# Parameter-only work of a state-space recurrence, moved into steps beside the feed-forward layer ahead of it, with its results in DRAM scratch

## The chip, the core and the metric

The kernel runs on one core of a Trainium2 chip. The metric is device time in microseconds (us) from launch to end. Three runs of the kernel before took 2534.7, 2537.55 and 2545.49 us; their median is 2537.55. The core's engines are named as in its profile: PE (TensorE, matrix multiplication), DVE (VectorE), ACT (ScalarE), POOL (GpSimd) and SP (SyncE, which issues most DMAs). Each works through its own instruction list in order and waits on semaphores where it needs another engine's result.

## The reference, cut to what matters

Two blocks of two layers each work on 512 tokens of 1024 features. The first block ends with a feed-forward layer (FFN) with a short convolution. The second block's first layer mixes a causal attention with forgetting and a diagonal state-space recurrence (S5); experts and a second mixer follow and are not touched.

```python
def _conv_ffn(x, norm_g, w_up, conv_w, conv_b, w_down):
    h = _rmsnorm(x, norm_g)
    up = h @ w_up                      # 1024 -> 2 * 2816
    gate, val = up[..., :D_FF], up[..., D_FF:]
    gate = conv3(gate, conv_w) + conv_b
    return (jax.nn.silu(gate) * val) @ w_down

def fox_s5_mixer(x, w_in, f_bias, a_re, a_im, log_dt, b_re, b_im, c_re, c_im, d_skip, w_glu, b_glu, w_out):
    q, k, v, f_logit, u = split(x @ w_in)
    att = forgetting_attention(q, k, v, f_logit + f_bias)
    y = s5_scan(u, a_re, a_im, log_dt, b_re, b_im, c_re, c_im, d_skip)
    y = jax.nn.gelu(y)
    y = y * jax.nn.sigmoid(y @ w_glu + b_glu)
    return jnp.concatenate([att, y], axis=-1) @ w_out

def s5_scan(u, a_re, a_im, log_dt, b_re, b_im, c_re, c_im, d_skip):
    dt = jnp.exp(log_dt)[:, None]
    mag = jnp.exp(a_re * dt)
    lb_re, lb_im = mag * jnp.cos(a_im * dt), mag * jnp.sin(a_im * dt)
    ...                                # z = (lb - 1) / a, bb = z * b, complex
    bu = einsum('bsgc,gpc->bsgp', u, bb)
    h = scan of h[t] = lb * h[t-1] + bu[t]
    y = einsum(h_re, c_re) - einsum(h_im, c_im)
    return y + d_skip * u
```

Everything in `s5_scan` down to `bb`, and every product of powers of lb with b or c, depends on parameters alone.

## The kernel before, in words

The program goes layer by layer: two mixers with an FFN behind each (f0, f1; f1 is "the second FFN"), then x0 (attention and S5), experts, a third mixer, experts. Features lie on partitions and the 512 tokens along the free dimension. Every product of two fp32 matrices is three matmuls of split operands: hi times hi, hi times lo, lo times hi (`mm3`, L153 to L155). `K.weight` (L140) loads a weight of up to 1 MB on SP's queue into one of two raw buffers; ACT makes its hi part in three pieces (whi, L147), and DVE or POOL in turn its lo part (wlo, L148). There are two buffers for hi and lo.

The FFN (function `ffn`) splits its normalised input into xh and xl, and computes 22 chunks of 128 gate and 128 value features, 48 matmuls of 128x512 each; after 11 chunks, 8 down products. Gate sums go to PSUM banks mm, value sums to sc, two banks of each kind. Per chunk DVE takes gt (mm times the row factor rb, L332), two taps of the convolution into y, v (sc times rb, then times y) and the lo split hl. rb comes from rms: PE sums squares, DVE makes rms and diag (L245), PE spreads it, ACT copies it as rb (L250).

The layer x0 (function `layer2`) takes tiles from a pool of 42 units of 128x512 and six tiles k4 of 128x1024. Its parts are generators that are woven by count: one side takes its steps of the other in proportion. On one side stand `s5_states` (parameters first: powers PW, phases, Er and Ei, bb and bs, four W by quads with PE transposes into Wt; then states) and eight steps of `s5_outputs` (four CP by quads, on POOL for quads 0 and 2 and on DVE for 1 and 3; then Kc by PE, 64 small matmuls at L1359 and L1360, which is copied out by ACT, and spread by 32 DMAs into the Toeplitz tiles T). On the other side stand the products of the layer: inputs u, forget gates, values, queries and keys (copied out of PSUM as fqk, L189). The state's outputs are hs (L1158 within a stacked complex product). After the weave PE does attention scores and the outputs' matmuls, T times U and CP times hs (L1380, L1381).

The order of instructions on each engine is not written by hand: a list scheduler places them by program order as priority, by its own estimates of time, and by when a buffer of a pool is free. An engine then executes that order as it stands.

Of the kernel before, what the change touches and what calls it, by code (L numbers as in the profile page):

```python
# [27 lines left out]
class Ctx:  # L28
# [137 lines left out]
    def rsqrt(self, v, n, name="rs"):  # L166
        """v: AP [P, n] fp32 (SBUF, > 0); returns tile [P, n] with v ** -0.5"""
# [17 lines left out]
    def copy(self, out, in_):  # L185
        """a copy out of PSUM, on ScalarE or (turns) by turns on ScalarE and VectorE"""
# [6 lines left out]
    def rsqrt_wide(self, ps, scale, eps):  # L193
        """(ps * scale + eps) ** -0.5 as an SBUF tile [P, 512]; ps in PSUM"""
# [10 lines left out]
    def silu2(self, x):  # L205
        """x <- 2 x / (1 + exp(-x)) = x (1 + tanh(x / 2)) of an SBUF tile; tanh shares a table with exp"""
# [4 lines left out]
    def sumsq_add(self, acc, src, first):  # L211
        """acc[P, 512] += src ** 2"""
# [8 lines left out]
    def colsum(self, acc):  # L221
        """column sums over partitions of acc [P, 512], as [P tokens, 4] in PSUM"""
# [5 lines left out]
    def rms_cols(self, acc, n, eps):  # L228
        """(column sums / n + eps) ** -0.5 as columns [P tokens, 4]; a step of Newton's method makes up for what the square root lacks"""
# [10 lines left out]
    def row_bcast(self, cols, name):  # L240
        """cols [P tokens, 4] -> SBUF tile [P, 512] holding the value of each token in every partition"""
# [11 lines left out]
    def split_into(self, hi, lo, src, scale=None, eng=None):  # L253
        """hi + lo = src * scale (scale: None or an AP [P, 1])"""
# [10 lines left out]
def weave(*parts):  # L265
    """runs generators side by side; parts: (generator, its number of steps)"""
# [15 lines left out]
def split_g(K, xT, g):  # L282
    """hi and lo tiles of xT * g; xT: 8 tiles [P, 512], g [P, 8]"""
# [9 lines left out]
def norm_cols(K, xT):  # L293
    """1 / rms(x) of 8 tiles [P, 512], as columns [P tokens, 4]"""
# [6 lines left out]
def norm_split(K, xT, g):  # L301
    """hi and lo tiles of xT * g, and the columns 1 / rms(x) [P tokens, 4]; the tiles of xT come one after the other"""
# [8 lines left out]
def ffn(K, xT, w_up, conv_w, conv_b, w_down, norm_g, tag):  # L311
    """xT (8 tiles [P, 512]) += conv_ffn(rmsnorm(xT)), in place.
    w_up [22, P, 2048] (8 k, gate 128 | val 128), conv_w [P, 22 * 3], conv_b [P, 22], w_down [2, 8, P, 1408], norm_g [P, 8]"""
# [5 lines left out]
    rb = K.row_bcast(rc, "rb")  # L319
    for half in range(2):  # L320
        hh, hl = [], []
        for j in range(11):
            f = half * 11 + j
            wh, wl = K.weight(w_up[f], 2048, nc.gpsimd if f < 2 else None)
# [22 lines left out]
        for d in range(8):  # L347
# [14 lines left out]
def lay_down(w):  # L362
    """[2816, 1024] -> [2, 8, 128, 1408]"""
# [3 lines left out]
def lay_col(v):  # L367
    """[n * 128] -> [128, n]"""
# [9 lines left out]
def sincos(K, sin, cos, ang, tmp):  # L378
    """sin and cos of ang (tiles or APs of one shape; tmp: three more, the first int32). ang is overwritten"""
# [12 lines left out]
def rope_tables(K, pos, inv):  # L392
    """pos [P, 4] int32, inv [P, 48]: sin and cos tiles [P, 4, 48] (16 columns for the 32-wide heads, 32 for the 64-wide)"""
# [15 lines left out]
def proj_T(K, src, n, nk, xh, xl):  # L409
    """src: DRAM [P, nk * n * 128] chunk, or hi and lo of one; yields PSUM tiles [P out, 512 tokens]"""  # L410
# [10 lines left out]
def proj_N(K, src, n, xh, xl):  # L421
    """src: DRAM [P, nk * n] chunk; yields t and the PSUM tile [P tokens, n] of each group of 128 tokens"""
# [12 lines left out]
def proj_few(K, src, n, xh, xl):  # L435
    """src: DRAM [P, 8 * n], n <= 128; the PSUM tile [n, 512 tokens]"""
# [7 lines left out]
def bc(ap, n):  # L444
    """[P, a] -> [P, a, n], the values repeated along the last axis"""
# [1824 lines left out]
```

## Time and profile before

| What | Value |
|---|---|
| runs, us | 2534.7, 2537.55, 2545.49 (median 2537.55) |
| profiled execution: span, us | 2542.8, first to last instruction |
| its own time | not given apart; at least the span |
| PE busy | 2292.3 us, 90% |
| DVE, ACT, POOL busy | 1488.8 (59%), 1064.3 (42%), 795.6 us (31%) |
| mean granted clock of PE | 0.946 |
| second FFN, about | 1032 to 1395 us |
| x0 up to the last key matmul | 1395 to 1566 us |

The trace is of one execution. Times in it count from its first instruction. A clock of 1.00 is PE's upper level, 2.4 GHz. "Idle before" is the time in which an engine stood still ahead of an instruction, with the one that released it.

### The profile page before, as it was taken

How to read it: one execution, taken by the hardware profiler on the slowest of the kernel's cores; microseconds unless marked ns; L12 is line 12 of the kernel's file. 1: busy time of each engine (PE TensorE's matmuls, PEld its weight loads, DVE VectorE, ACT ScalarE, POOL GpSimd, SP SyncE). 2: the span in 40 equal slices, each digit the busy share in tenths (PEclk: the TensorE clock that was granted, in tenths of full speed). 3: DMA queues.
4: the chain of work that ended last, by engine and by line, in shares of the span. 5: the costliest groups of instructions: out<-in, count | busy, mean ns of one | idle time of the engine just before them, and what ended most of it. 6: DMA issues, size and time to landing. Idle time of an engine off the chain costs nothing. (4 is left out here: it accounts for less than half of the span.)

```text
span 2542.8 us, 32031 instructions
## 1 busy us (share of the span) xinstructions
PE 2292.3 (90%) x12404; PEld 1858.3 (73%) x12404; DVE 1488.8 (59%) x2713; ACT 1064.3 (42%) x1802; POOL 795.6 (31%) x582
## 2 busy tenths in 40 slices
PE   7999899999998999999999978995985899997892
PEld 6845658888886988788888866675875788886781
DVE  6256756525545447752554784657765545576766
ACT  4233455323334323532333223534665444445563
POOL 5321203222222322322222151216543312154444
PEclk9999899999998999999999998996988899998996
DMA  3111202223221121223222212124986322245883
GB/s 142 67 35 35 76 1 83 89 95 107 84 93 67 67 67 67 83 89 101 100 84 91 71 40 67 51 99 157 326 308 221 119 83 77 73 176 210 298 321 139
DMA packets 59432, 289.89 MB, mean 114 GB/s; under 512 B 12576, under 2 KB 13600, under 8 KB 33664
## 3 DMA queue, kind: packets, MB, share of 16 engines
q1 hardware_dynamic: 48944, 265.51, 30.0%
q0 software_dynamic: 6912, 16.79, 1.9%
q10 hardware_dynamic: 3408, 5.39, 0.6%
q8 instruction: 101, 1.65, 0.3%
q14 instruction: 67, 0.55, 0.1%
HBM read 271.79 MB, written 23.07 MB: 116 GB/s over the span
## 5 line engine op out<-in xcount | busy, mean ns | idle before, releaser
L148 POOL TENSOR_TENSOR wlo<-wraw,whi 128x683 fp32r<-128x683 f32 (+8 forms) x317 | 557.2, 1785 | 1266.2 <-ACT whi L147 1215.6
L147 ACT ACTIVATE whi<-wraw 128x683 fp32r<-128x683 f32 (+9 forms) x627 | 474.3, 818 | 386.5 <-PE mm L154 127.1
L148 DVE TENSOR_TENSOR wlo<-wraw,whi 128x683 fp32r<-128x683 f32 (+9 forms) x310 | 342.8, 1144 | 90.0 <-ACT whi L147 83.5
L153 PE MATMUL mm<-xh,whi 128*128 128x512 f32 (+2 forms) x576 | 230.5, 400 | 19.4 <-ACT xh L260 8.7
L155 PE MATMUL mm<-xh,wlo 128*128 128x512 f32 (+2 forms) x576 | 227.4, 395 | 0.4 <-POOL wlo L148 0.3
L154 PE MATMUL mm<-xl,whi 128*128 128x512 f32 (+2 forms) x576 | 227.7, 395 | 0.0
L153 PE MATMUL mm<-whi,xh 128*128 128x256 f32 x576 | 175.6, 305 | 14.8 <-DVE xs L504 5.1
L155 PE MATMUL mm<-whi,xl 128*128 128x256 f32 x576 | 174.1, 303 | 0.0
L154 PE MATMUL mm<-wlo,xh 128*128 128x256 f32 x576 | 172.5, 300 | 0.0
L153 PEld LDWEIGHTS mm<-xh,whi 128*128 128x128 f32 (+2 forms) x576 | 107.8, 187 | 50.3 <-ACT xh L260 9.5
L161 PE MATMUL mm<-whi,Xh 128*128 128x256 f32 x512 | 134.4, 298 | 4.7 <-ACT whi L147 4.7
L155 PE MATMUL sc<-xh,wlo 128*128 128x512 f32 x352 | 138.0, 392 | 0.0
L154 PE MATMUL sc<-xl,whi 128*128 128x512 f32 x352 | 137.0, 389 | 0.0
L153 PE MATMUL sc<-xh,whi 128*128 128x512 f32 x352 | 137.0, 389 | 0.0
L153 PEld LDWEIGHTS mm<-whi,xh 128*128 128x128 f32 x576 | 121.0, 210 | 20.3 <-issue 10.7
L162 PE MATMUL mm<-whi,Xl 128*128 128x256 f32 x512 | 131.6, 292 | 0.3
L154 PEld LDWEIGHTS mm<-xl,whi 128*128 128x128 f32 (+2 forms) x576 | 107.5, 187 | 28.9 <-DVE xl L261 2.5
L155 PEld LDWEIGHTS mm<-xh,wlo 128*128 128x128 f32 (+2 forms) x576 | 107.6, 187 | 27.2 <-POOL wlo L148 1.0
L154 PEld LDWEIGHTS mm<-wlo,xh 128*128 128x128 f32 x576 | 121.2, 210 | 0.7 <-issue 0.2
L155 PEld LDWEIGHTS mm<-whi,xl 128*128 128x128 f32 x576 | 121.0, 210 | 0.3
L161 PEld LDWEIGHTS mm<-whi,Xh 128*128 128x128 f32 x512 | 101.3, 198 | 6.5 <-ACT whi L147 5.8
L162 PEld LDWEIGHTS mm<-whi,Xl 128*128 128x128 f32 x512 | 101.4, 198 | 1.1 <-DVE Xl L258 0.9
(785 smaller groups left out, 5310.3 us busy)
## 6 DMA issues: line engine op xcount, KB each, us to landing
wraw<-in_f_up SPq DMA_DIRECT2D x44, 1024.0 KB, 4.9
wraw<-in_m_w_up SPq DMA_DIRECT2D x32, 1024.0 KB, 6.9
wraw<-in_m_w_gate SPq DMA_DIRECT2D x32, 1024.0 KB, 5.7
wraw<-in_m_w_down SPq DMA_DIRECT2D x32, 1024.0 KB, 7.3
wraw<-in_f_down SPq DMA_DIRECT2D x32, 704.0 KB, 4.1
dy<-Y SPq DMA_DIRECT2D x32, 512.0 KB, 3.5
wraw<-in_w_out SPq DMA_DIRECT2D x8, 1024.0 KB, 4.8
wraw<-in_x_out SPq DMA_DIRECT2D x8, 1024.0 KB, 5.0
```

The source lines that it names most:

```text
L147: nc.scalar.activation(out=hi[:, a:b], in_=raw[:, a:b], func=ACT.Copy)
L148: eng.tensor_tensor(out=lo[:, a:b], in0=raw[:, a:b], in1=hi[:, a:b].bitcast(F32), op=ALU.subtract)
L153: nc.tensor.matmul(out, ahi, bhi, start=first, stop=False)
L154: nc.tensor.matmul(out, ahi, blo, start=False, stop=False)
L155: nc.tensor.matmul(out, alo, bhi, start=False, stop=last)
L161: nc.tensor.matmul(out, a[k][0], b[k][0], start=k == 0, stop=False)
L162: nc.tensor.matmul(out, a[k][1], b[k][0], start=False, stop=False)
```

## The change

The parameter work of S5 becomes a generator of its own, `s5_params`, and the second FFN calls one step of it ahead of each of its 22 up chunks (`next(beside, None)`). Its results go to DRAM scratch: Er and Ei (in two halves), Wt, CP, and the Toeplitz tiles, which are filled with zeros by 8 DMAs and then with Kc by 32. x0 loads them back: 8 loads of Wt with 256 KB each, Er and Ei with 512 KB each, 4 of T with 512 KB, 8 of CP with 256 KB, all on SP's queue. W for quads 0 and 2 moves from DVE to POOL; the diagonal term is added in 2 operations per quad instead of 8; Kc has one buffer instead of two and its sums use the PSUM banks sm instead of mm. In x0 the product for the inputs u now runs first and alone, and only then the weave of the 11 state steps with the other products.

```diff
-def ffn(K, xT, w_up, conv_w, conv_b, w_down, norm_g, tag):
+def ffn(K, xT, w_up, conv_w, conv_b, w_down, norm_g, tag, beside=None):
...
     rb = K.row_bcast(rc, 'rb')
+    beside = beside() if beside else iter(())
     for half in range(2):
...
             f = half * 11 + j
+            next(beside, None)
             wh, wl = K.weight(w_up[f], 2048, nc.gpsimd if f < 2 else None)
...
-def s5_states(K, A, uc, S):
+def s5_params(K, A, D):
...
+    work = lambda n: small.tile([P, 512], F32, tag='sw', name=n, bufs=6)
...
+    zero = work('zero')
+    G.memset(zero, 0.0)
+    for quad in range(4):
+        for i in range(2):
+            nc.sync.dma_start(D['t'][quad, :, 4 * i:4 * i + 4], zero.rearrange('p (a b) -> p a b', b=P))
+    yield
     PW = c.tile([P, 2, 9, 16], F32, name='PW')
...
         cmul(V, PW[:, 0, j], PW[:, 1, j], l1, (PW[:, 0, j - 1], PW[:, 1, j - 1]), t1, t2)
+    yield
     nr, zr, zi, den = (t('nr'), t('zr'), t('zi'), t('den'))
...
+    for hf in range(2):
+        prs = slice(hf * 8, hf * 8 + 8)
+        Er, Ei = (work(n).rearrange('p (a b) -> p a b', a=8) for n in ('Er', 'Ei'))
...
+            cmul(V, Er[:, :, L:2 * L], Ei[:, :, L:2 * L], (Er[:, :, 0:L], Ei[:, :, 0:L]), b, T1[:, :, :L], T2[:, :, :L])
+            L *= 2
+        for n, E in (('er', Er), ('ei', Ei)):
+            nc.sync.dma_start(D[n][:, prs], E)
+        yield
...
     for quad in range(4):
         prs = slice(quad * 4, quad * 4 + 4)
-        Ws.append([K.u('Wr'), K.u('Wi')])
+        Ws = [work('Wr'), work('Wi')]
...
-        cmul(V, *(x4(w) for w in Ws[quad]), pw, tuple((wide(b[:, prs].unsqueeze(2)) for b in (bbr, bbi))), x4(K.u('a1')), x4(K.u('a2')))
+        cmul((G, V)[quad % 2], *(x4(w) for w in Ws), pw, tuple((wide(b[:, prs].unsqueeze(2)) for b in (bbr, bbi))), x4(work('a1')), x4(work('a2')))
         yield
-    for quad in range(4):
-        out = []
-        for w in Ws[quad]:
+        for i, w in enumerate(Ws):
             pt = K.sm()
             for j in range(4):
                 nc.tensor.transpose(pt[:, j * P:(j + 1) * P], w[:, j * P:(j + 1) * P], K.ident)
-            o = K.u('Wt')
+            o = work('Wt')
             K.copy(o, pt)
-            out.append(o)
-        Wt.append(out)
+            nc.sync.dma_start(D['wt'][quad, :, i], o)
...
+    for quad in range(4):
+        prs = slice(quad * 4, quad * 4 + 4)
+        CP = [work('CP0'), work('CP1')]
...
+        cmul_stack((G, V)[quad % 2], [x4(w) for w in CP], pw, tuple((wide(v3(b)[:, prs].unsqueeze(2)) for b in (cr, cn))), x4(work('a1')), x4(work('a2')), conj=True)
+        for par in range(2):
+            nc.sync.dma_start(D['cp'][quad, :, par], CP[par])
+        yield
+        Kc = small.tile([16, 8, P], F32, tag='Kc', name='Kc', bufs=1)
...
+        for s in range(8):
+            nc.sync.dma_start(D['t'][quad, s * 16:s * 16 + 16, :, s * 16:P], Kc[:, :, 0:P - s * 16])
+        yield
+
+def s5_states(K, D, uc, S):
...
+    for quad in range(4):
+        Wt.append([K.u('Wt'), K.u('Wt')])
+        for i in range(2):
+            nc.sync.dma_start(Wt[quad][i], D['wt'][quad, :, i])
+    Er, Ei = (k4(K, n).rearrange('p (a b) -> p a b', a=16) for n in ('Er', 'Ei'))
+    nc.sync.dma_start(Er, D['er'])
+    nc.sync.dma_start(Ei, D['ei'])
...
-def s5_outputs(K, A, S, yT):
+def s5_outputs(K, D, S, yT):
...
     for quad in range(4):
...
+        CP.append([K.u('CP0'), K.u('CP1')])
         for par in range(2):
...
+            nc.sync.dma_start(CP[quad][par], D['cp'][quad, :, par])
+        T.append(k4(K, 'T').rearrange('p (g n) -> p g n', g=8))
+        nc.sync.dma_start(T[quad], D['t'][quad])
...
-    outputs = s5_outputs(K, A, st, yT)
-    weave((chain(s5_states(K, A, uc, st), islice(outputs, 8)), 22), (chain(inputs(), forget(), to_N(K, xT, hN), values(), queries_keys()), 33))
+    outputs = s5_outputs(K, D, st, yT)
+    for _ in inputs():
+        pass
+    weave((s5_states(K, D, uc, st), 11), (chain(forget(), to_N(K, xT, hN), values(), queries_keys()), 25))
...
-        ffn(K, xT, A['f1_up'], A['f1_cw'], A['f1_cb'], A['f1_down'], A['f1_g'], 'f1')
+        K.m8 = K.gconst.tile([P, 16], F32, name='m8')
+        ffn(K, xT, A['f1_up'], A['f1_cw'], A['f1_cb'], A['f1_down'], A['f1_g'], 'f1', lambda: s5_params(K, A, D))
```

What the scheduler makes of it shows in three places. The first is DVE at the start of the second FFN, in the order before; rms and diag stand there together, and the first gt follows.

```order
L233 TENSOR_SCALAR rmsv<-sm 128x4
L234 RECIPROCAL rmsr<-rmsr 128x4
L235 TENSOR_TENSOR rmsa<-rmsr 128x4
L236 TENSOR_TENSOR rmsa<-rmsa,rmsv 128x4
L237 SCALAR_TENSOR_TENSOR rmsr<-rmsa,rmsr 128x4
L245 TENSOR_SCALAR diag<-ident,rmsr 128x128 x4
L332 TENSOR_TENSOR gt<-mm,rb 128x512
L341 TENSOR_TENSOR v<-sc,rb 128x512
L332 TENSOR_TENSOR gt<-mm,rb 128x512
L335 SCALAR_TENSOR_TENSOR y<-gt,pk_117,y 128x511
```

Now, on the same engine and from the rms rows on (t and PW are tiles of the chain of powers):

```order
L1149 TENSOR_TENSOR t_8409<-PW 128x16
L1150 TENSOR_TENSOR t_8410<-PW 128x16
L234 TENSOR_TENSOR rmsa<-rmsr 128x4
L1151 TENSOR_TENSOR PW<-t_8409,t_8410 128x16
L235 TENSOR_TENSOR rmsa<-rmsa,rmsv 128x4
L1146 TENSOR_TENSOR t_8409<-PW 128x16
L1147 TENSOR_TENSOR t_8410<-PW 128x16
L236 SCALAR_TENSOR_TENSOR rmsr<-rmsa,rmsr 128x4
L1148 TENSOR_TENSOR PW<-t_8409,t_8410 128x16
L244 TENSOR_SCALAR diag<-ident,rmsr 128x128 x4
L1149 TENSOR_TENSOR t_8409<-PW 128x16
L1150 TENSOR_TENSOR t_8410<-PW 128x16
```

Rows of the chain of powers stand among the rms rows and behind diag; 32 rows of the chain stand between diag and the first gt.

The second place is SP's queue at the end of x0's products. In the order before, the output weight's first load stands between the DMAs that spread Kc:

```order
L1367 DMA T<-Kc 16x8x48
L1367 DMA T<-Kc 16x8x32
L1367 DMA T<-Kc 16x8x16
L140 DMA wraw<-in_x_out 128x2048
L1367 DMA T<-Kc 16x1024
L1367 DMA T<-Kc 16x8x112
```

Now the loads of CP stand there, two output weight loads ahead of them (the first two of eight CP loads are shown; the other two output weight loads follow the eighth):

```order
L139 DMA wraw<-in_w_fk 128x2048 x2
L139 DMA wraw<-in_w_glu 128x1024 x2
L139 DMA wraw<-in_x_out 128x2048 x2
L1389 DMA CP_12403<-dcp 128x512
L1389 DMA CP_12404<-dcp 128x512
```

The DMAs that spread Kc are gone from this place, and the first CP load stands behind the second load of the output weight.

The third place is PE at the end of the query and key products. Before (the number behind CP is the tile's):

```order
L1359 MATMUL mm<-cs,bs 16x16
L1360 MATMUL mm<-CP_11966,bs 16x112
L1560 MATMUL sc<-cTh,idr 128x512
L1560 MATMUL sc<-cTl,idr 128x512
L1565 MATMUL sc<-fqk 128x128
L1566 LDWEIGHTS idb
L1566 MATMUL sc<-cm,idb 128x128
L1380 MATMUL mm<-T,U 64x128
L1381 MATMUL mm<-CP_11813,hs_11551 64x128
```

Now:

```order
L154 MATMUL mm<-xh,wlo 128x512
L1589 LDWEIGHTS idb
L1589 MATMUL sc<-cm,idb 128x128
L1403 MATMUL mm<-T,U 64x128 x2
L1583 MATMUL sc<-cTh,idr 128x512
L1583 MATMUL sc<-cTl,idr 128x512
L1588 MATMUL sc<-fqk 128x128
L1589 LDWEIGHTS idb
L1589 MATMUL sc<-cm,idb 128x128
L765 MATMUL tr<-ident,fs 128x128
L1404 MATMUL mm<-CP_12403,hs_11982 64x128
L1403 MATMUL mm<-T,U 64x128
```

The last Kc matmuls are gone, and the first matmul that reads a loaded CP stands directly behind a transpose (tr) of a softmaxed block.

## Rows read from the trace of the kernel before

**Rows 1.** Page, part 1: busy time, share of the span, instructions.

```profile
PE 2292.3 (90%) x12404; PEld 1858.3 (73%) x12404; DVE 1488.8 (59%) x2713; ACT 1064.3 (42%) x1802; POOL 795.6 (31%) x582
```

**Rows 2.** Waits of PE, 1385 to 1700 us: us in total, times, longest.

```profile
PE mm L1359 <- ACT fqk L189: 13.4, 3, 12.3
...
PE mm L153 <- ACT fqk L189: 8.6, 1, 8.6
...
PE sc L1274 <- ACT U L189: 1.2, 1, 1.2
```

**Rows 3.** Busy time by stretch; its first row names the columns.

```profile
core 0: us, PE busy (x) PEld busy (x) DVE busy (x) ACT busy (x) POOL busy (x), PEclk, DMA share, GB/s
1040.00:1080.00 40.00, 40.00 (x180) 32.87 (x179) 24.29 (x41) 17.97 (x26) 10.69 (x6) 1.00 0.29 102
1390.00:1440.00 50.00, 48.39 (x222) 46.41 (x221) 47.42 (x193) 10.20 (x26) 7.29 (x7) 1.00 0.15 48
1500.00:1520.00 20.00, 11.37 (x41) 8.35 (x41) 19.77 (x14) 2.70 (x4) 18.18 (x13) 0.83 0.16 53
1520.00:1540.00 20.00, 7.16 (x49) 5.06 (x47) 17.09 (x22) 4.12 (x7) 9.86 (x6) 0.66 0.15 40
```

**Rows 4.** Timeline of ACT: start, duration, instruction, [idle before <- releaser].

```profile
1514.76 0.60 ACT L189 ACTIVATE fqk<-mm 128x512 f32<-128x512 f32 x1 [12.63 <-DVE hs L1158]
...
1534.12 0.60 ACT L189 ACTIVATE fqk<-mm 128x512 f32<-128x512 f32 x1 [18.76 <-DVE CP L1158]
```

**Rows 5.** Timeline of DVE, 1520 to 1532 us, same columns.

```profile
1520.03 2.14 DVE L1155 TENSOR_TENSOR a<-PW,cr 128x512 f32<-128x512 f32 x1
...
1531.29 0.69 DVE L1154 TENSOR_TENSOR a<-PW,cn 128x512 f32<-128x512 f32 x1
```

**Rows 6.** Timeline of PE behind the first gap.

```profile
1515.41 0.79 PE L153 MATMUL mm<-xh,whi 128*128 128x512 f32 x1 [8.56 <-ACT fqk L189]
...
1518.45 0.39 PE L154 MATMUL mm<-xl,whi 128*128 128x512 f32 x1
...
1518.68 0.40 PE L155 MATMUL mm<-xh,wlo 128*128 128x512 f32 x1
```

**Rows 7.** Timeline of DVE at the start of the second FFN.

```profile
1047.49 0.88 DVE L245 TENSOR_SCALAR diag<-ident,rmsr 128x128 f32<-128x128 f32 x4
1054.56 0.69 DVE L332 TENSOR_TENSOR gt<-mm,rb 128x512 f32<-128x512 f32 x1 [6.19 <-ACT rb L250]
```

**Rows 8.** Timeline of DVE, small operations of the parameter chain.

```profile
1396.03 1.51 DVE L1129 TENSOR_TENSOR eaq<-eaq,ear 128x16 f32<-128x16 f32 x1
...
1397.57 1.57 DVE L1130 TENSOR_SCALAR eaq<-eaq 128x16 f32<-128x16 f32 x1
...
1404.35 0.17 DVE L1142 TENSOR_TENSOR t<-PW 128x16 f32<-128x16 f32 x1
...
1411.20 0.17 DVE L1147 TENSOR_TENSOR PW<-t,t 128x16 f32<-128x16 f32 x1
```

**Rows 9.** Timeline of POOL at the start of the second FFN.

```profile
1032.36 6.28 POOL L148 TENSOR_TENSOR wlo<-wraw,whi 128x682 fp32r<-128x682 f32 x3 [9.59 <-ACT whi L147]
1049.43 4.89 POOL L148 TENSOR_TENSOR wlo<-wraw,whi 128x682 fp32r<-128x682 f32 x3 [10.79 <-ACT whi L147]
```

**Rows 10.** Timeline of PE around the end of queries and keys.

```profile
1565.60 0.39 PE L155 MATMUL mm<-xh,wlo 128*128 128x512 f32 x1
...
1569.30 0.48 PE L1565 MATMUL sc<-fqk 64*128 64x128 f32 x2
...
1573.57 0.33 PE L761 MATMUL tr<-ident,fs 128*128 128x128 f32 x1
```

**Rows 11.** Timeline of SP, the output weight's load behind it.

```profile
1567.71 0.33 SPq L140 DMA_DIRECT2D wraw<-in_x_out  x1
```

**Rows 12.** DMA issues: KB each, median us to landing.

```profile
wraw<-in_x_out SPq DMA_DIRECT2D x8, 1024.0 KB, 5.0
...
dx<-hN SPq DMA_DIRECT2D x16, 256.0 KB, 2.0
```

More of the change, by code (lines that the diff above doesn't have):

```diff
@@ L1 @@
 from contextlib import ExitStack
-from itertools import islice
 import numpy as np
@@ L354, in ffn @@
             nc.vector.tensor_tensor(out=xT[d], in0=xT[d], in1=ps, op=ALU.add)
+    for _ in beside:
+        pass
 def lay_up(w):
@@ L1173, in s5_states @@
     t = lambda n, dt=F32: small.tile([P, 16], dt, tag="sv" + n, name=n, bufs=1)
+    work = lambda n: small.tile([P, 512], F32, tag="sw", name=n, bufs=6)
+    two = lambda x: (x[:, :256], x[:, 256:])
+    v3 = lambda a: a.rearrange("p (a b) -> p a b", b=16)
+    (br, bi), (cr, cn) = two(K.h("br")), two(K.h("cr"))
+    for o, n in ((br, "s5_br"), (bi, "s5_bi"), (cr, "s5_cr"), (cn, "s5_ci")):
+        nc.scalar.dma_start(o, A[n])
     dt, _ = exp_acc(K, ldt, "dt")
@@ L1181, in s5_states @@
     nc.scalar.activation(out=hs, in_=th, func=ACT.Sin, scale=0.5)
+    zero = work("zero")
+    G.memset(zero, 0.0)
+    for quad in range(4):
+        for i in range(2):
+            nc.sync.dma_start(D["t"][quad, :, 4 * i:4 * i + 4], zero.rearrange("p (a b) -> p a b", b=P))
+    yield
     PW = c.tile([P, 2, 9, 16], F32, name="PW")
@@ L1201, in s5_states @@
     V.tensor_tensor(out=zi, in0=zi, in1=den, op=MU)
-    m8, ph = t("m8"), c.tile([P, 2, 16], F32, name="ph")
+    m8, ph = K.m8, (t("ph0"), t("ph1"))
     V.tensor_tensor(out=m8, in0=mag, in1=mag, op=MU)
@@ L1261, in s5_states @@
                 nc.tensor.transpose(pt[:, j * P:(j + 1) * P], w[:, j * P:(j + 1) * P], K.ident)
-            o = K.u("Wt")
+            o = work("Wt")
             K.copy(o, pt)
-            out.append(o)
-        Wt.append(out)
+            nc.sync.dma_start(D["wt"][quad, :, i], o)
+    V.tensor_scalar(out=cn, in0=cn, scalar1=-1.0, scalar2=None, op0=MU)
+    cs_ = K.h("cs")
+    cS = [v3(cs_[:, i * 256:i * 256 + 256]) for i in range(2)]
+    for par in range(2):
+        r = slice(par * 64, par * 64 + 64)
+        V.tensor_copy(out=cS[par][0:64], in_=v3(cr)[r])
+        V.tensor_copy(out=cS[par][64:128], in_=v3(cn)[r])
@@ new lines, in s5_params @@
+    dcol = K.load(A["s5_d"])
+    dg = small.tile([16, 8, 16], F32, tag="dg", name="dg", bufs=1)
+    for quad in range(4):
+        prs = slice(quad * 4, quad * 4 + 4)
+        CP = [work("CP0"), work("CP1")]
+        pw = tuple(wide(PWv[:, i, prs, 1:9].unsqueeze(3)) for i in range(2))
+        cmul_stack((G, V)[quad % 2], [x4(w) for w in CP], pw, tuple(wide(v3(b)[:, prs].unsqueeze(2)) for b in (cr, cn)), x4(work("a1")), x4(work("a2")),
+                   conj=True)
+        for par in range(2):
+            nc.sync.dma_start(D["cp"][quad, :, par], CP[par])
+        yield
+        Kc = small.tile([16, 8, P], F32, tag="Kc", name="Kc", bufs=1)
+        for par in range(2):
+            ps = K.sm()
+            for pair in range(4):
+                pg = quad * 4 + pair
+                o = ps[0:16, pair * P:(pair + 1) * P]
+                nc.tensor.matmul(o[:, 0:16], bbS[par][:, pg], cS[par][:, pg], start=True, stop=True)
+                nc.tensor.matmul(o[:, 16:128], bbS[par][:, pg], CP[par][:, pair * P:pair * P + 112], start=True, stop=True)
+            K.copy(Kc[:, par::2, :], ps[0:16, :].rearrange("p (a b) -> p a b", b=P))
+        V.tensor_tensor(out=dg, in0=K.ident[0:16, 0:16].unsqueeze(1).to_broadcast([16, 8, 16]), in1=bc(dcol[:, quad * 8:quad * 8 + 8], 16), op=MU)
+        V.tensor_tensor(out=Kc[:, :, 0:16], in0=Kc[:, :, 0:16], in1=dg, op=AD)
+        for s in range(8):
+            nc.sync.dma_start(D["t"][quad, s * 16:s * 16 + 16, :, s * 16:P], Kc[:, :, 0:P - s * 16])
+        yield
@@ new lines, in s5_states @@
+def s5_states(K, D, uc, S):
+    nc = K.nc
+    V = nc.vector
+    Wt = []
+    for quad in range(4):
+        Wt.append([K.u("Wt"), K.u("Wt")])
+        for i in range(2):
+            nc.sync.dma_start(Wt[quad][i], D["wt"][quad, :, i])
+    Er, Ei = (k4(K, n).rearrange("p (a b) -> p a b", a=16) for n in ("Er", "Ei"))
+    nc.sync.dma_start(Er, D["er"])
+    nc.sync.dma_start(Ei, D["ei"])
+    R0 = [K.u("R0").rearrange("p (a b) -> p a b", b=64) for _ in range(2)]
+    for i in range(2):
+        V.tensor_copy(out=R0[i], in_=bc(K.m8[:, i * 8:i * 8 + 8], 64))
+        V.memset(R0[i][:, :, 0:1], 0.0)
@@ L1312, in s5_states @@
         yield
[L1313 to L1316 removed]
+    S.update(Ug=Ug, Hs=Hs)
+def s5_outputs(K, D, S, yT):
     nc = K.nc
[L1319 to L1368 removed]
@@ L1370, in s5_outputs @@
+    Ug, Hs = S["Ug"], S["Hs"]
+    CP, T = [], []
+    for quad in range(4):
+        CP.append([K.u("CP0"), K.u("CP1")])
+        for par in range(2):
+            nc.sync.dma_start(CP[quad][par], D["cp"][quad, :, par])
+        T.append(k4(K, "T").rearrange("p (g n) -> p g n", g=8))
+        nc.sync.dma_start(T[quad], D["t"][quad])
     for b in range(2):
@@ L2213, in program @@
         K.start_turns(1, 0)
-        ffn(K, xT, A["f1_up"], A["f1_cw"], A["f1_cb"], A["f1_down"], A["f1_g"], "f1")
+        K.m8 = K.gconst.tile([P, 16], F32, name="m8")
+        ffn(K, xT, A["f1_up"], A["f1_cw"], A["f1_cb"], A["f1_down"], A["f1_g"], "f1", lambda: s5_params(K, A, D))
         hN = [[None, None] for _ in range(4)]
```

94 lines of the change are left out of this document (20 added, 74 removed).

## The prediction, made before the change was timed

> **What bounds the kernel now.** I read the page's busy shares first: PE is busy 2292.3 of 2542.8 us [rows 1]. So TensorE is the resource, and a change gains only where PE stands idle, or runs at its lower clock, in the stretch that is changed. The stretch is x0, the attention layer from 1395 us on, where the recurrence's parameter work sits now. PE's waits there come next [rows 2]: 13.4 us before the matmuls that make Kc (L1359) and 8.6 us before query and key matmuls (L153), both released by ACT's copies fqk, and 1.2 us for U. The third view is the table of stretches [rows 3]. From 1500 to 1540 PE is busy 11.4 and 7.2 of 20 us, while DVE is busy 19.8 and 17.1, and POOL 18.2 in the first of them. ACT's rows say who holds whom: the two fqk copies that PE waits for started after 12.63 and 18.76 us of idle, released by DVE's hs and CP [rows 4]. Tiles come from one pool of units, and the copy needs a unit that DVE has not let go. DVE is slow there because POOL works on CP at the same time: a 128x512 product takes 2.14 us at 1520.03 and 0.69 us at 1531.29, after POOL's last CP [rows 5]. In the same table the second FFN (1040 to 1080) has PE busy all 40 us, with DVE 24.3 and POOL 10.7: room on the two engines, none on PE.
>
> **What leaves x0.** The parameter work on DVE and POOL leaves, so hs and the copies come early. I count both big gaps as gone: 13.4 + 8.6 = 22.0 us. Of the waits for U, 1.2 us, I count half, 0.6, since U is still copied by ACT but with less around it.
>
> After each gap PE runs slower for a while. The first 7 matmuls after the first gap take from 1515.41 to 1518.45, 3.04 us; from there the spacing is 0.23 us, 1.61 us for seven [rows 6]. They run at the 1.2 GHz level instead of 2.4: the granted clock in that stretch is 0.83, in the next 0.66 [rows 3]. So 1.4 us behind the first gap, and I take the same behind the second: 2.8. Together the gain is 22.0 + 0.6 + 2.8 = 25.4 us; its bounds are 20 (the gaps shrink but a shorter fqk wait stays) and 27.
>
> The transposes of W and the Kc matmuls move from x0 to the FFN. PE is in demand in both, so their busy time is the same term on both sides: zero.
>
> **What the start of the FFN pays.** In DVE's order small rows of the parameter chain now stand in four places: ten among the xl rows, 32 between these and the rms rows (powers PW), six among the rms rows, and 32 between diag and the first gt (PW, zr, zi, phases). Before, DVE idled 6.19 us ahead of that gt, waiting for rb [rows 7]. Undisturbed, the same chain goes from 1404.35 to 1411.20 in 44 rows, 0.16 us each [rows 8]. Beside a split on POOL one of them takes 1.51 to 1.57 us [rows 8], and POOL's split for the third chunk runs from 1049.43 for 4.89 us, exactly in this place [rows 9]. So four rows held at 1.55 are 6.2 us, the other 28 at 0.16 are 4.5, the six ahead of diag 1.0: 11.7 us, less the 6.19 of idle, delay gt by 5.5 us at the worst. At the best they delay it by nothing: 32 rows at 0.16, 5.1 us, fit the hole. The gt frees the PSUM bank that PE needs for its third chunk at about the same time, so I see no slack, and take 4. The 32 rows ahead of rms lie beside PE's first chunk, in a hole of their own, since rms waits for a sum that PE makes after it. The xl rows pay too: the ten rows are put among them while POOL's split of 1032.36 runs for 6.28 us [rows 9], and ACT's Sin, with a table load, stands among the xh rows that PE's first chunk needs. I take 2, from 0 to 5. With a slow restart of 1.4 us as above, the start costs 7 us, from 0 to 13.
>
> **What the rest of the FFN pays.** DVE's moved work is at most its busy time in the three stretches of x0, 47.4 + 19.8 + 17.1 = 84 us [rows 3], over 22 chunks of 11 us, 3.8 each. The FFN's own share is 24.3 of 40, 6.7 per chunk. 10.5 of 11 would just fit on average, but Er and Ei crowd into chunks 2 to 6, and DVE then lags by a few us. PSUM's two banks per kind allow a lag of more than a chunk. What has less room is a transpose in PE's order that waits for a W made late: W's second half of quad 0 waits for the last Ei row, whose place is behind the gt of the chunk before. I take 2 us, from 0 to 12 (28 instructions of CP and W on POOL, each holding DVE for about 1.5, are 43 us of holding; a quarter of that on the path would be the 12).
>
> The new DMAs on SP (8 of zeros, 4 of Er and Ei, 8 of Wt, 8 of CP, 32 of Kc) wait for their producers in front of weight loads. A load has a chunk of time in hand, and this costs nothing unless DVE is a chunk late; that case is in the 12.
>
> **What the loads in x0 pay.** Wt, Er, Ei and T are issued ahead of the weights for queries and keys. T's first use comes after all of these, and the first use of Wt behind 192 matmuls on the inputs, 44 us at 0.23. These hide. CP's loads do not: in SP's order they stand behind the second load of the output weight. That load waits for the split of the last gate weight, which waits for PE's last query and key matmul, E = 1565.8 us with the spacing of 0.23 behind its start [rows 10]: before, that load is issued at 1567.71 [rows 11], E + 1.9, and lands after 5.0 us [rows 12], at E + 6.9. The CP loads go through the same queue behind it; a transfer of 256 KB (here a store) takes 2.0 us [rows 12], so the first lands at about E + 7 to E + 8, and the eighth at E + 9 to E + 12. PE, in order, has one pair of scores to do between E and the first CP matmul, and a transpose that waits for a softmax: before, scores at 1569.30 and the transpose at 1573.57 [rows 10], 4.3 us, which T and CP matmuls filled. Now nothing fills it. PE then stands from about E + 1.7 to E + 7.5, 5.8 us, plus 1.4 for the slow restart, plus about 1 for later CPs: 8 us. The bounds are 5 (only the softmax wait and a slow restart) and 14 (every CP waited for until E + 12).
>
> **A rule of the Trainium skill against this.** The held small operations above are a row of this case: 0.17 us alone, 1.55 beside POOL [rows 8]. The Trainium skill, "GPSIMD Engine Reference", section "Key points", says that GpSimd shares its SBUF interfaces with VectorE and contends with instructions that have two SBUF inputs or run in a 2-port mode. The trace agrees, also for the row at 1397.57, which has a single tensor input. By that rule gt and the first v, which read PSUM, would go unhindered, and all CP and W work on POOL would hold the FFN's other DVE rows; its mechanism, priced from rows, is rival C.
>
> **Sum.** -25.4 + 7 + 2 + 8 = -8.4 us on the profiled execution: a span of 2542.8 becomes 2534. That span is 5 us above the median of the three runs, 2537.55; the difference carries over, so 2537.55 - 8.4 = 2529 us.
>
> **Rivals.**
> A. The whole gain stays: the scheduled order meets real times, gt comes when rb does, and CP's loads land while PE still has scores. The cost is then 0 + 0 + 5 and the gain 25 to 27: 20 to 22 us, 2516. For it: the hole of 6.19 us before gt, and 40% idle DVE in the FFN [rows 3, 7]. Against it: the place of the CP loads behind a weight load, which the order fixes.
>
> B. The forecast: part of the gain is given back at the FFN's start and at CP's loads; 2529, own range 2523 to 2536.
>
> C. Slower: POOL's W and CP in the FFN hold DVE, one DVE instruction per POOL instruction. Then DVE's 6.7 + 3.8 us per chunk grow by the holding. Some 28 POOL instructions and about 20 small rows beside splits at 1.4 us extra are 43 + 28 = 71 us over the roughly 12 chunks that carry steps, 5.9 per chunk: 16.4 of 11 us, and PE waits 5.4 us in each chunk past what the two PSUM banks absorb (about 16 us). 12 x 5.4 - 16 = 49 at full force; with half of the holding beside idle DVE it is 12 x 2.4 - 16 = 13, and the kernel is slower than before once it passes 25.4 - 7 - 8 = 10.4 us. I price it at 24 us in the place of 2: net +14, 2551. For it: 2.14 against 0.69 us [rows 5]. Against it: the four 128x512 products and the stretched rows are spread over a stage where DVE stands idle 16 of 40 us [rows 3].
>
> D. The change does not shorten x0: the fqk copies wait for units for another reason, for example because hs are still late behind the scans. Then the 17 us are paid and some 5 of the gain remain, since POOL no longer slows hs: net +12, 2550. ACT's second wait ended with DVE's CP [rows 4], which is gone; I give it little.
>
> **Chances.** A 0.32, B 0.50, C 0.12, D 0.06. A change within 0.5% (12.7 us, 2524.9 to 2550.2) is what a measurement of this kernel can hardly tell from none. Of B some 0.10 falls below 2524.9, of C and D about half lies above 2550.2. So faster 0.40, same 0.51, slower 0.09. The range 2511 to 2546 leaves out 0.05 below and 0.14 above.
>
> **What would show it.** Right, if PE's waits in x0 no longer name fqk, and the stretches from 1500 to 1540 show PE full at clock 1.0; if the first gt of the FFN starts 3 us or more later after rb than before; if after PE's last key matmul there is a wait of 5 to 8 us for CP, released by a DMA. Rival A shows by no wait for CP over 2 us and an FFN as long as before. Rival C shows as waits of PE for wlo, gt or W in the FFN, with DVE over 90% busy in its stretches. The prediction is wrong if the FFN grows by over 20 us, or if x0 keeps a wait of more than 8 us for a copy.

## The result, and the profile after

The changed kernel takes 2552.09 us (median of 14 runs, 2548.4 to 2556.42); the kernel before took 2538.38 us in the same session (14 runs, 2527.56 to 2545.72). The ratio is 1.0054 with a 95% interval of 1.004 to 1.0068: slower by 0.5%, 13.7 us by the medians. The forecast was 2529 us with a range of 2511 to 2546. It had the sign wrong.

The two profiled executions have spans of 2542.8 and 2549.4 us, 6.6 us apart. The difference by stages is read from the first matmul of each:

| Stage, us | before | after | difference |
|---|---|---|---|
| up to the second FFN's first matmul | 1031.7 | 1032.2 | +0.5 |
| second FFN, first 11 up chunks | 122.3 | 142.8 | +20.5 |
| its first 8 down chunks | 60.7 | 69.2 | +8.5 |
| second 11 up chunks | 119.7 | 126.6 | +6.9 |
| second 8 down chunks | 60.7 | 60.8 | +0.1 |
| x0, to the last key matmul | 170.6 | 131.9 | -38.7 |
| from there to the transposes of x0's normalised output | 138.2 | 148.9 | +10.7 |
| from there to the end | 839.0 | 837.0 | -2.0 |

All rows that follow are of the executions profiled; a change of a few us in stretches that no edit touches is their spread.

What was to leave x0 left it. The stretches after, in the columns of [rows 3] (PE, PEld, DVE, ACT, POOL busy, granted clock, DMA share, GB/s), with the first half of the FFN and the stretch behind the last key matmul added:

```profile
1032.00:1200.00 168.00, 152.96 (x652) 122.89 (x653) 150.78 (x321) 60.77 (x97) 70.41 (x46) 0.95 0.29 97
1500.00:1520.00 20.00, 20.00 (x202) 19.15 (x201) 16.44 (x19) 6.28 (x12) 6.48 (x3) 1.00 0.16 53
1520.00:1540.00 20.00, 20.00 (x116) 16.42 (x115) 2.37 (x4) 3.78 (x6) 4.90 (x3) 1.00 0.24 79
1563.00:1583.00 20.00, 14.74 (x134) 11.46 (x133) 6.28 (x21) 7.48 (x18) 0.00 (x0) 0.74 0.44 158
```

The same 168 us of the FFN before:

```profile
1032.00:1200.00 168.00, 168.00 (x739) 137.57 (x738) 84.95 (x115) 62.87 (x97) 45.89 (x27) 1.00 0.27 91
```

The two stretches from 1500 on, where PE stood half idle [rows 3], are full at clock 1.0. But in the FFN, where PE had no gap, it is busy 153 of 168 us, and DVE went from 85 to 151 us. All that moved to DVE, 85.8 us over the whole FFN (180.0 before, 265.8 after), is close to the 84 that the prediction took. PE's waits after, from 1020 to 1440 us (us in total, times, longest):

```profile
PE sm L1272 <- POOL Wi L1151: 5.6, 1, 5.6
PE mm L152 <- DVE xT L1058: 3.6, 1, 3.6
PE mm L152 <- ACT hh L256: 3.4, 1, 3.4
PE mm L152 <- DVE gt L334: 2.5, 1, 2.5
PE mm L153 <- DVE xl L260: 1.5, 1, 1.5
PE sm L1272 <- DVE Wi L1151: 0.9, 1, 0.9
```

and from 1440 to 1680, where both fqk rows of [rows 2] are gone:

```profile
PE mm L1404 <- DMA CP<-dcp: 3.0, 2, 2.8
PE tr L765 <- DVE fs L759: 2.4, 2, 1.4
PE sc L1588 <- DVE fs L1592: 1.6, 1, 1.6
PE mm L1403 <- ACT fqk L188: 1.2, 1, 1.2
```

The costliest wait of the FFN is 5.58 us at a transpose of Wi, the second of the two tiles of a W. It can be followed through three engines, PE, POOL and DVE, in that order:

```profile
1126.62 1.12 PE L1272 MATMUL sm<-ident,Wi 128*128 128x128 f32 x4 [5.58 <-POOL Wi L1151]
```

```profile
1110.01 1.64 POOL L1150 TENSOR_TENSOR a<-PW,bb 128x512 f32<-128x512 f32 x1
1125.30 1.26 POOL L1151 TENSOR_TENSOR Wi<-a,a 128x512 f32<-128x512 f32 x1 [13.65 <-DVE Ei L1151]
```

```profile
1124.75 0.41 DVE L1151 TENSOR_TENSOR Ei<-et 128x256 f32<-128x256 f32 x1
```

POOL had all operands of Wi at 1111.7. It stood 13.65 us because Wi goes into one of six scratch tiles, and the tile it gets is freed by the last row of the doubling of Ei, which DVE reached at 1124.75. PE's next 128x512 matmuls stood in order behind the transposes. DVE is busy 9.2 to 9.9 of every 10 us from 1050 to 1140, so every row in its queue is late by then.

The wait for hh, 3.4 us, has another maker, as far as the rows show. hh comes from v, v from gt, and gt stands in DVE's queue behind rows of the chunk before, which run beside POOL's CP. Some of POOL's rows and DVE's:

```profile
1165.85 3.32 POOL L1162 TENSOR_TENSOR CP<-a,a 64x512 f32<-64x512 f32 x2
```

```profile
1166.35 1.66 DVE L339 SCALAR_TENSOR_TENSOR y<-gt,pk,y 128x511 f32<-128x511 f32 x1
1167.93 0.68 DVE L343 TENSOR_TENSOR v<-sc,rb 128x512 f32<-128x512 f32 x1
...
1179.76 0.75 DVE L339 SCALAR_TENSOR_TENSOR y<-gt,pk,y 128x511 f32<-128x511 f32 x1
```

The last row is the same work one chunk later, while POOL stands still. Between 1164.9 and 1175.7 two rows for y, one for v and the three of a weight's split take 9.0 us; where POOL does no CP (the second experiment) the same rows take 3.9.

The start of the FFN went nearly as priced. DVE's rows there, after, which answer to [rows 7, 8]:

```profile
1051.62 0.87 DVE L244 TENSOR_SCALAR diag<-ident,rmsr 128x128 f32<-128x128 f32 x4
...
1053.41 1.57 DVE L1149 TENSOR_TENSOR t<-PW 128x16 f32<-128x16 f32 x1
1054.90 1.70 DVE L1150 TENSOR_TENSOR t<-PW 128x16 f32<-128x16 f32 x1
1056.63 1.57 DVE L1151 TENSOR_TENSOR PW<-t,t 128x16 f32<-128x16 f32 x1
...
1061.79 0.68 DVE L334 TENSOR_TENSOR gt<-mm,rb 128x512 f32<-128x512 f32 x1
```

Three rows are held beside POOL's split, and gt starts 10.2 us after diag instead of 7.1. diag itself is 3.7 us later, counted from the FFN's first matmul. The third chunk's first matmul comes 30.4 us after the FFN's first instead of 24.4, and the fourth's, behind a slow restart, 42.8 instead of 35.2: 7.6 us.

Behind the last key matmul (1563.54) SP issues the loads of CP from 1566.03 on, and PE waits first for a softmax, then for the load:

```profile
1568.33 0.48 PE L765 MATMUL tr<-ident,fs 128*128 128x128 f32 x1 [1.02 <-DVE fs L759]
1571.65 0.47 PE L1404 MATMUL mm<-CP,hs 128*64 128x128 f32 x1 [2.85 <-DMA CP<-dcp]
```

### The profile page after: what moved, and what is told of

The parts are those of the page before. It is cut to its first block, busy times and chain, and to the rows that moved or that the text cites. A ratio compares the mean times of both kernels' runs of the same rounds, so it can differ in the third digit from the quotient of the medians.

```text
span 2549.4 us, 32122 instructions
## 1 busy us (share of the span) xinstructions
PE 2304.2 (90%) x12404; PEld 1865.6 (73%) x12404; DVE 1503.8 (59%) x2723; ACT 1060.1 (42%) x1795; POOL 807.3 (32%) x591
## 5 line engine op out<-in xcount | busy, mean ns | idle before, releaser
L146 ACT ACTIVATE whi<-wraw 128x683 fp32r<-128x683 f32 (+9 forms) x627 | 474.0, 817 | 384.6 <-PE mm L153 135.0
L152 PE MATMUL mm<-whi,xh 128*128 128x256 f32 x576 | 176.6, 307 | 13.6 <-DVE xs L508 5.0
L154 PEld LDWEIGHTS mm<-xh,wlo 128*128 128x128 f32 (+2 forms) x576 | 108.1, 188 | 27.8 <-POOL wlo L147 1.2
```

Of the source, the lines that this page charges most:

```text
L146: nc.scalar.activation(out=hi[:, a:b], in_=raw[:, a:b], func=ACT.Copy)
L152: nc.tensor.matmul(out, ahi, bhi, start=first, stop=False)
L154: nc.tensor.matmul(out, alo, bhi, start=False, stop=last)
```

## The experiments

The theory after the result had two rivals for the FFN's loss. Theory 1: DVE is full in the first up half, and all that stands in its queue is late. Theory 2: POOL's work on W and CP holds DVE, one DVE instruction per POOL instruction. Each kernel is the changed one with one edit, unless said otherwise. Its median stands beside 2552.09, the median of the changed kernel; "FFN" is the length of the second FFN in its one profiled execution (before 363.3, after 399.5). The kernel before had medians of 2542.98, 2540.93 and 2539.97 in the three sessions below, so a difference of a few us between sessions is not read.

**Without the doubling of Er and Ei.**

```diff
-        V.tensor_copy(out=Er[:, :, 0], in_=ph[0][:, prs])
-        V.tensor_copy(out=Ei[:, :, 0], in_=ph[1][:, prs])
-        L = 1
+        V.tensor_copy(out=Er, in_=bc(ph[0][:, prs], 64))
+        V.tensor_copy(out=Ei, in_=bc(ph[1][:, prs], 64))
+        L = 64
         while L < 64:
```

> Leaves out the doubling of Er and Ei (72 small DVE instructions in the first half of the second FFN; four copies stand in their place, so the recurrence's decay factors are not the reference's). Theory 1 (DVE is full in the first up half and everything behind it in its queue is late): PE's waits for Wi (6.5 us) and for hh (3.4 us) in the FFN vanish with their slow restarts, time 8 to 14 us below the changed kernel (2552), about 2540. Theory 2 (POOL's W and CP hold DVE): the same POOL instructions are there, so within 4 us of the changed kernel.

Measured: 2540.63 us, ratio to before 1.0003 (0.9991 to 1.0014); FFN 390.1. PE's waits for Wi are gone; those for xT (3.6), hh (3.4) and gt (2.5) stand. The doubling cost 9.4 us in the FFN, all of it through the wait for W; hh is late for another reason; POOL's CP is still there.

**All of W and CP on DVE.**

```diff
-        cmul((G, V)[quad % 2], *(x4(w) for w in Ws), pw, ...
+        cmul(V, *(x4(w) for w in Ws), pw, ...
-        cmul_stack((G, V)[quad % 2], [x4(w) for w in CP], pw, ...
+        cmul_stack(V, [x4(w) for w in CP], pw, ...
```

> W and CP of quads 0 and 2 on DVE instead of POOL. Theory 1 (DVE is full): DVE gets some 28 more instructions of 0.69 to 1.3 us, 20 us more, and the FFN gets longer, 3 to 12 us slower than the changed kernel. Theory 2 (POOL holds DVE one instruction each): without those POOL instructions the DVE rows run at 0.69 us, the waits for Wi and hh shrink, 6 to 12 us faster than the changed kernel.

Measured: 2537.99 us, ratio 0.999 (0.9975 to 1.0005); FFN 389.0. PE's waits, 1010 to 1440 us:

```profile
PE mm L152 <- DVE xT L1058: 3.6, 1, 3.6
PE mm L152 <- DVE gt L334: 2.5, 1, 2.5
PE sm L1272 <- DVE Wi L1151: 2.3, 1, 2.3
PE mm L153 <- DVE xl L260: 1.5, 1, 1.5
```

More rows on DVE made the FFN 10.5 us shorter. Theory 1, put as the load of DVE alone, is wrong. The 10.5 us have two parts. The first 8 down chunks are 5.6 us shorter (63.6 against 69.2), where hh's wait is gone and DVE's rows run at their short times: that fits theory 2. The first 11 up chunks are 4.9 us shorter, where Wi's wait fell to 2.3 us, but not because Wi came sooner:

```profile
1125.71 1.54 DVE L1151 TENSOR_TENSOR Wi<-a,a 128x512 f32<-128x512 f32 x1
```

It ends 94.7 us behind the FFN's first matmul, and in the changed kernel, on POOL, 94.4. In both it follows the last row of Ei. What changed is PE's order: between the transposes of Wr and those of Wi it has 24 of the FFN's matmuls instead of 6, and 18 more at 0.23 us are 4.1 us of work where PE stood.

**Steps from the third chunk on.**

```diff
-            next(beside, None)
+            if f >= 2:
+                next(beside, None)
```

> The steps begin at the third up chunk instead of the first, so no parameter row stands among xl, rms and diag. Theory 1: PE's waits for xT (1.3 more than before), xl (1.5) and gt (2.5) vanish with one or two slow restarts of 1.4 us, 6 to 9 us below the changed kernel; the wait for Wi stays or moves two chunks later. Theory 2: the start costs nothing by POOL, no change over 3 us.

Measured: 2535.72 us, ratio 0.9972 (0.9958 to 0.9986); FFN 387.5. The median is 16.4 us below the changed kernel, more than the 6 to 9 expected, and 12.0 of it are in the FFN, but not where they were expected. The waits at the start stayed: xT 3.6, gt 2.3, xl 1.5. What shrank is Wi, to 0.6, and hh, to nothing. The scheduler still put the ready parameter rows into DVE's free places ahead of gt. Wi is no earlier either:

```profile
1126.06 1.29 POOL L1152 TENSOR_TENSOR Wi<-a,a 128x512 f32<-128x512 f32 x1 [13.67 <-DVE Ei L1152]
```

```profile
1143.15 0.60 PE L1273 MATMUL sm<-ident,Wi 128*128 128x128 f32 x4
```

It ends 94.5 us behind the FFN's first matmul, after the same wait for the scratch tile, but its transposes now stand behind 432 of the FFN's matmuls instead of 342, at 110.3 us, and find it ready. So a late W costs nothing where PE's order asks for it late enough. Wi's wait of 0.6 is that of a later quad; W and CP of the later quads moved to the second half, and with them what held hh.

**CP's loads written earlier.** In `s5_outputs` the four pairs of loads are taken out; they stand at the end of `s5_states`:

```diff
+    CP = []
+    for quad in range(4):
+        CP.append([K.u("CP0"), K.u("CP1")])
+        for par in range(2):
+            nc.sync.dma_start(CP[quad][par], D["cp"][quad, :, par])
-    S.update(Ug=Ug, Hs=Hs)
+    S.update(Ug=Ug, Hs=Hs, CP=CP)
```

> The eight loads of CP are written at the end of the state steps, ahead of the output weight's loads on SP's queue. If the wait behind the last key matmul is the load's place in the queue: PE's wait for CP (3.0 us) goes, and with it a slow restart, 3 to 6 us below the changed kernel. If the softmax chain in front of the transpose sets it: within 2 us of the changed kernel, with the wait renamed.

Measured: 2537.32 us, ratio 0.998 (0.997 to 0.999); FFN 399.4, as after. SP now issues the loads at 1546.38, and the first matmul with CP starts 0.7 us behind the last key matmul (8.1 before the edit):

```profile
1565.23 0.39 PE L154 MATMUL mm<-xh,wlo 128*128 128x512 f32 x1
...
1565.89 0.40 PE L1406 MATMUL mm<-CP,hs 128*64 128x128 f32 x4
```

From the last key matmul to the transposes of x0's output it takes 135.3 us, against 148.9. Over the first 20 us PE has no gap, and its granted clock is 1.00, where it was 0.74. But not all of the 13.6 us are the loads' place. From 30 to 60 us behind the last key matmul the clock was 0.69 after and 1.00 here, and there it differs between kernels that do not differ in this stretch. All experiments on the changed kernel, those that follow too:

| Loads of CP | clock, 30 to 60 us behind | stretch, us |
|---|---|---|
| late: changed kernel, no doubling, all on DVE, doubling last | 0.69 to 0.73 | 147.6 to 149.1 |
| late: from the third chunk, held | 0.94, 0.94 | 143.4, 143.0 |
| early: combined, both of the last edits | 0.79, 0.77 | 139.7, 140.7 |
| early: this one, combination on DVE, transposes later | 1.00, 0.94, 1.00 | 135.3, 132.2, 135.0 |

At like clock, by the means, the early loads are worth 8 to 9 us, nearly three times the wait of 3.0 us that the profile puts down to them; kernels with the higher clock there are another 5 to 6 us shorter. What sets that clock was not traced, and a gain of that size in this stretch is not put down to an edit in the FFN.

**Steps held behind the chunk before.** Besides the later start, each step's DVE rows get an order edge to the first v of the chunk before:

```diff
-            next(beside, None)
+            if f >= 2:
+                with K.tc.issue_after(held):
+                    next(beside, None)
...
-            nc.vector.tensor_tensor(out=v, in0=pv, in1=rb, op=ALU.mult)
+            held = nc.vector.tensor_tensor(out=v, in0=pv, in1=rb, op=ALU.mult).ins
```

> The steps begin at the third up chunk and each step's DVE rows must stand behind the v of the chunk before, so none can be put among xl, rms and diag at the FFN's start. If these rows cost what the trace says (third chunk's first matmul 30.4 us after the FFN's first instead of 24.4, its restart slow): 7 to 10 us below the changed kernel. If the start is late for another reason, such as the zero DMAs or the Sin on ACT: within 3 us of it.

Measured: 2532.55 us, ratio 0.9968 (0.9954 to 0.9982); FFN 390.0. The median is 19.5 us below the changed kernel, twice what was expected; in the profile 9.5 of it are in the FFN and 5.9 in the stretch behind the last key matmul (see the table). The start is as before: the third chunk 24.3 us after the first, the fourth 35.2, and no wait for xT, xl or gt. What is left:

```profile
PE sm L1274 <- DVE Wr L1150: 5.6, 1, 5.6
PE sm L1274 <- POOL Wr L1150: 3.0, 1, 3.0
PE mm L152 <- ACT xh L259: 0.7, 1, 0.7
```

The two costs are separate: the start, 7.6 us, comes from the rows ahead of gt, and W's lateness stays without it.

**The doubling last.** The block that makes Er and Ei is moved behind W, CP and Kc; nothing else changes.

> The doubling of Er and Ei is made after W, CP and Kc instead of ahead of them; all instructions stay. If PE's wait for Wi is a wait of POOL for a scratch tile that the doubling's last row frees: both waits for Wi (6.5 us) and a slow restart of 1.4 to 3 us go, 8 to 11 us below the changed kernel. If DVE's total load is what counts (the same rows, only later): the time moves by less than 4 us and the wait appears at Kc or at a gt. If POOL's holding is: no change either.

Measured: 2542.72 us, ratio 1.0004 (0.999 to 1.0019); FFN 395.2. The median is 9.4 us below the changed kernel, as expected if the scratch tile was the cause, but the execution profiled is the longest of the 12 (2548.6), and its FFN is only 4.3 us shorter. The wait of POOL's Wi for a scratch tile is gone, and with it PE's 5.6 us. But two waits for W on DVE (1.4 each), one for a weight split and one for xl (1.7) came:

```profile
PE mm L152 <- ACT whi L146: 2.9, 1, 2.9
PE sm L1257 <- DVE Wi L1151: 2.9, 2, 1.4
```

In this profile half of the gain was given back, as theory 1 has it. Neither theory holds alone: a transpose waits for W, and W is late by whichever of the scratch tile, the queue on DVE and the queue on POOL is last.

**The kernel before, inputs first.** Only the order of x0's weave is changed, in the kernel before:

```diff
-    weave((chain(s5_states(K, A, uc, st), islice(outputs, 8)), 22), (chain(inputs(), forget(), ...), 33))
+    for _ in inputs():
+        pass
+    weave((chain(s5_states(K, A, uc, st), islice(outputs, 8)), 22), (chain(forget(), ...), 25))
```

> The kernel before with only the order of x0 changed: the product for the inputs runs first and alone, the parameter work stays in x0. If x0's gain came from the parameter work leaving: within 10 us of before, with PE still waiting 8 us or more for fqk. If it came from the order: 15 us or more below before.

Measured: 2537.41 us, ratio to before 0.9991 (0.9977 to 1.0005): no change; x0 takes 170.8 us, against 170.6. PE's waits from 1385 to 1600 moved, but hardly shrank: in x0 up to the last key matmul PE stands 21.9 us, against 24.6. fqk is named for 7.1 of it, a little under the 8 expected:

```profile
PE sc L1560 <- DVE vt L1145: 8.6, 1, 8.6
PE mm L1359 <- ACT fqk L189: 6.1, 2, 5.6
PE sc L1274 <- ACT U L189: 2.6, 1, 2.6
```

So x0's gain needs the parameter work's leaving; the new order alone brings nothing. The leaving without the new order was not run.

**Three edits combined:** the doubling last, the steps held, CP's loads early.

> The doubling last, the steps held behind the chunk before, and CP's loads ahead of the output weight's. If the three costs are separate they add up: 9 + 9 + 15 us below the changed kernel (15 is what the loads alone gave), that is 2515 to 2523, and about 1% below before. If they share a cause (one late DVE queue): 2525 to 2532.

Measured: 2520.45 us, ratio 0.9927 (0.9908 to 0.9946); FFN 382.9. 31.6 us below the changed kernel. In the FFN the edits add up: 16.6 us shorter, 9.5 and 4.3 alone. Over the whole kernel they do not: the medians gave 19.5, 9.4 and 14.8 us alone, 43.7 together. The held steps alone had 5.9 us from the stretch behind the last key matmul, which their edit does not touch.

**The combination with all of W and CP on DVE.**

> The combination of the last run with W and CP of all quads on DVE. If POOL's holding of DVE is what still costs in the FFN: the wait for W (4.0 us in the last run) goes, 3 to 6 us below it, 2514 to 2518. If DVE's load is: about 20 us more work on DVE, PE waits longer for W, 2 to 6 us above it.

Measured: 2512.01 us, ratio 0.9897 (0.9879 to 0.9916), but FFN 384.6, longer by 1.7, with PE waiting 4.5 us for W on DVE in place of 4.0 for POOL. The gain lies behind the last key matmul (964.7 against 976.4 us), where nothing was edited: 7.5 of the 11.7 us in the stretch of the table, at clock 0.94 against 0.79, the rest later. So it says nothing for POOL's holding in the FFN.

**The combination with transposes one step later,** and the doubling in smaller steps, some of them beside the down chunks:

```diff
         yield
+        yield
         for i, w in enumerate(Ws):
...
             L *= 2
+            if L in (8, 32):
+                yield
...
+            if half == 0:
+                next(beside, None)
             wh, wl = K.weight(w_down[half, d], 1408)
```

> The same combination with one empty step between each W and its transposes, the doubling in six steps instead of two, and steps in the first half's down chunks too. If what still costs is PE standing in its order at a transpose whose W is late: the wait for W goes with its slow restart, 4 to 7 us below 2520, and the FFN is within 3 us of 363.3 + 11.7 us of moved PE work. If DVE is full over the whole up half: another wait (wlo, gt or hh) takes its place and the time stays within 2 us.

Measured: 2512.42 us, ratio 0.9888 (0.987 to 0.9907); FFN 380.7. The waits for W are down to 0.5 us:

```profile
PE mm L152 <- ACT hh L256: 1.2, 1, 1.2
PE mm L153 <- DVE hl L257: 0.8, 1, 0.8
PE mm L152 <- ACT xh L259: 0.7, 1, 0.7
PE sm L1262 <- POOL Wi L1155: 0.5, 1, 0.5
```

This version is 1.1% faster than before and 40 us below the changed kernel. Of the 8.0 us that it has over the combination, only 2.2 are in the FFN; 4.7 are in the stretch of the table, at clock 1.00 against 0.79. Three edits are in it, and which of them brought the 2.2 was not tried apart.

**Both of the last edits.**

> Both of the edits of this call together. If the late transposes are the whole rest, this equals the kernel with the empty step (within 2 us) and POOL does not matter; if POOL's holding matters too, it is 2 to 4 us faster.

Measured: 2518.38 us, ratio 0.9908 (0.989 to 0.9927); FFN 381.7, with a wait of 2.9 us for Wi on DVE. The time is 6.0 us above the kernel with the empty step, which neither expectation had, but the FFN is only 1.0 longer; 5.7 are in the stretch of the table, at clock 0.77 against 1.00. Without POOL's share the transposes are late again, one step's delay or not. Taking POOL's instructions away brings nothing once the steps are placed: theory 2 is not what costs in the FFN there.

## Why the prediction was wrong, step by step

- **x0's gain** (25.4 us, bounds 20 to 27) had the mechanism right and the size nearly. x0 is 38.7 us shorter. Of this the PE work that moved is about 11: in the second up half, where PE does not wait, three groups of Kc matmuls make it 6.9 us longer, 2.3 each, and three of the four groups stood ahead of the last key matmul; eight groups of four transposes at 0.5 add 4. The rest is 27.8, just past the upper bound: PE stood 24.6 us in x0 before and 0.2 after, and ran slow behind its gaps. The order alone gives nothing, so the cause is the parameter work's leaving.
- **One row was misread on the way.** The product of 2.14 us at 1520.03 [rows 5] ran beside POOL's split of a weight (1517.56 to 1523.66), not beside its CP; beside CP, from 1525.74, such products took 1.48 and 1.75 us. It changes no term of the sum. In the bound of 12 a quarter of 43 is 10.8, and in the chances A and the part of B make 0.42, not 0.40.
- **Moved PE work as zero** was right: it left x0 and the stretch behind, and came back in the FFN, about 13 us with the fourth group of Kc.
- **The FFN's start** (7 us) was right: 7.6, with three held rows where four were put. Holding the steps back removed it.
- **The rest of the FFN** (2 us, bounds 0 to 12) is the step that failed. The FFN is 36.2 us longer; less 13.2 of moved work and 7.6 of the start, 15.4 remain, of which 10.8 are waits (Wi 5.6 and 0.9, hh 3.4, wlo 0.9) and the others slow restarts. By the experiments 9.4 of it went with the doubling of Er and Ei, and 5.6, in the down chunks, when POOL's W and CP went to DVE; in the kernel with the transposes a step later and the steps spread, about 4 remain. The step named the place, a transpose in PE's order that waits for a late W behind the last row of Ei, and then priced it at nearly nothing. The work on DVE was sized rightly, but the average it leaned on, over 22 chunks, 3.8 us each, is not how the work lies: in the first 11 up chunks DVE is busy 134.7 us, against 73.4 before: 5.6 more on 6.7 a chunk, over the 11 that a chunk lasts. PSUM's two banks did absorb gt's lag, as said, but the transposes had no such slack, and the scratch tiles tied W to the doubling.
- **CP's loads** (8 us, bounds 5 to 14) were right in place, cause and size: 8 to 9 by the experiments at like clock. The single wait for CP of 5 to 8 us that was to show it did not come; it was 3.0, behind waits for a copy (1.2) and a softmax. Between the two profiles the stretch is 10.7 us longer, though a group of Kc (2.3) left it, so 13.0 stand in the sum. The prediction had no term for the 4 to 5 above the loads. They stand beside a lower clock 30 to 60 us behind the last key matmul, 0.69 against 0.83 before; that it is their cause is not shown.
- **The sum** with measured terms is -27.8 + 7.6 + 15.4 + 13.0 = +8.2, against +6.6 between the profiles and +13.7 between the medians. The difference of the last two lies in the spread of the executions.
- **Rival C** (slower, POOL's holding, 0.12) had the sign and nearly the time, 2551, but by luck: its mechanism is seen in the held rows at the start and, read from the rows, in hh's wait, about a third of the 15.4, and not in the longest wait, for Wi, which is no earlier with POOL's share on DVE. Its sign, waits of PE for W with DVE over 90% busy, came, but could not tell it from the doubling.

## What to carry to other kernels

Work that is moved beside a full TensorE has to fit chunk by chunk, not on average: read how many chunks the steps reach, and put the matmuls that consume a moved result at least a step behind its maker, since TensorE waits in order. A list scheduler fills free places with ready low-priority rows, so a step that must not start early needs an order edge. A load that a later stage needs first should be written ahead of prefetches that wait for the stage before it.

## What the runs showed of the hardware

A wait is dearer than its row. With CP's loads early PE stood 5.5 us in the stretch behind the last key matmul instead of 10.0, and at like clock further on the stretch is 8 to 9 us shorter: over its first 20 us the granted clock had been 0.74 and went to 1.00. A group of four 128x128 transposes took 1.12 us behind a wait of 5.58 us, and 0.63 behind one of 0.87. Beside POOL's CP a DVE row with both inputs in SBUF took 1.66 us instead of 0.75, and one that reads PSUM (v, at 1167.93) 0.68, as without POOL.
